# A hybrid decoder block on one core: the second 512 tokens of the gate stage in other groups, and the opening in a written order

## The chip, the cores and the metric

The kernel runs on one core of a Trainium2 chip. The time is the device time of one execution in microseconds (us), the median of several. The engines are called as in the profile: PE is the matrix engine (PEld its weight loads), DVE the vector engine, ACT the scalar engine, POOL the GpSimd engine, SP the engine from whose queue the kernel issues nearly all its DMAs. PSUM is the memory that matmuls write, SBUF the memory that all engines read and write.

## The reference

One layer on 1024 tokens of 1024 channels. What matters here is the first projection and everything behind the MLP:

```python
z = rms_norm(h, norm_mix_g[l])
proj = z @ w_in[l]
...
z = rms_norm(h, norm_ple_g[l])
gate = jax.nn.sigmoid(z @ w_ple_gate[l] + b_ple_gate[l])
h = h + gate * (p[l] @ w_ple_proj[l])
return rms_norm(h, norm_final_g)
```

w_ple_gate is 1024 x 1024, w_ple_proj 256 x 1024. All arithmetic is in 32-bit floats.

## The kernel before

Activations lie transposed: 128 channels on the partitions, tokens along the row. H[0] to H[7] are the eight blocks of the residual stream. Each operand of a matmul is split in two rounded parts, hi and lo (`split`: ACT writes hi, DVE subtracts it to get lo; for weights `load_weights` does the same and can hand the subtraction to POOL). A product is then three matmuls: hi x hi, hi x lo, lo x hi (`mm`).

The first RMS norm divides behind the matmul, since the divisor is one number per token: PE multiplies by the gain-scaled x, and the rows that drain PSUM multiply by R, the reciprocal root mean square. `Norm.add` squares a block on ACT and adds it up on DVE, `sums` adds over partitions with two matmuls by a matrix of ones (n_ps in the profile), `rstd` makes the reciprocal root.

**Opening.** For each block k of x, SP loads H[k] and 384 columns of the first weights (wl), ACT and DVE split both, and PE runs 18 matmuls into ps_l. The squares go along: blocks 0 to 2 are added at k = 2, after that one per block. The loads of two small tables (`tables`) and a chain of small DVE rows on four columns (`softplus`, tile sp) are issued at k = 2. Up to there, instructions marked by `pin` keep the order of the program; from then on (`in_order.clear()`) the scheduler chooses.

**Gate stage.** For each output block o and each group of tokens, PE runs 24 matmuls of the gate (ps_e; k over eight blocks, three products) and 6 of the projection (ps_j, or the other half of a ps_e tile). `ple_out` then drains them: DVE multiplies by R (L1055), ACT takes the sigmoid, DVE multiplies by the projection (L1061) and adds to H (L1062), and `fin.add` squares the result for the final norm (ACT, DVE). The groups are tokens 0 to 511, 512 to 767 and 768 to 1023; each runs over all eight outputs in the order of ORDER:

```python
GROUPS = (slice(0, 512), slice(512, 768), slice(768, 1024))
ORDER = ((0, 1, 2, 3, 4, 5, 6, 7), (2, 3, 4, 5, 6, 7, 0, 1), (0, 1, 4, 5, 6, 7, 2, 3))
```

In the third group, `ple_in_normed` multiplies the operand by R before it is split (DVE L928, ACT L177, DVE L178), so that the sigmoid reads PSUM itself (L1053). The gate's weights for outputs 4 to 7 stay in SBUF (wg4 to wg7 in tiles B); those of 0 to 3 go through a ring of two and are loaded and split again: 0 and 1 in the second group, 2 and 3 in the third, with the subtraction on POOL (FETCH).

`finish` forms the final norm of a group while the next one runs: `fin.sums`, `rstd`, then one DVE row per output that multiplies by gain and reciprocal root (L1079), and a store for four outputs. DONE and LAST say after which output which rows come. `finish_last` does this for the third group at the end, where ACT has already multiplied by the gain (`gain`, L1084).

An output's ps_e and ps_j take turns between one two-bank tile (two of them) and two one-bank tiles (four, which the sums also use).

Of the kernel before, what the change touches and what calls it, by code (L numbers as in the profile page):

```python
# [13 lines left out]
P = 128  # L14
S = 1024
# [7 lines left out]

SOON = 20

AHEAD = ((0,), (1, 2), (3,), ())
IN = {("P5", 2): (0, 1), ("P5", 3): (2, 3), ("P3", 0): (4, 5), ("P3", 1): (6, 7)}
LATER = ((), (0, 1), (2, 3), (4, 5), (6, 7), (), ())
GROUPS = (slice(0, 512), slice(512, 768), slice(768, 1024))
NT = D // P  # L30

ORDER = ((0, 1, 2, 3, 4, 5, 6, 7), (2, 3, 4, 5, 6, 7, 0, 1), (0, 1, 4, 5, 6, 7, 2, 3))

DONE = (((), (), (0,), (1,), (2,), (3,), (4,), (5,)), ((6,), (7,), (), (), (), (), (), ()))
LAST = ((), (), (0, 1), (2, 3), (4, 5), (6, 7), (), ())
FETCH = ((0, 1, 2, 3), (0, 1), (2, 3))
NLRU = 4
NPOOL = 4
WINDOWS = (2, 4, 8, 16)
# [18 lines left out]
def block_kernel(  # L58
# [86 lines left out]
    def f32(ap):  # L145
        return ap.bitcast(F32)
# [6 lines left out]
    def got(ps):  # L153
        if ps.shape[-1] > HALF:
            return ps.rearrange("p (b j a) -> p b a j", b=2, a=2)
        return ps.rearrange("p (j a) -> p a j", a=2)

    def by(x, ps):
        if ps.shape[-1] > HALF:
            return x.rearrange("p (b a j) -> p b a j", b=2, a=2)  # L160
        return x.rearrange("p (a j) -> p a j", a=2)

    def col(name, i):
        c = COLS[name] + i
        return vecs[:, c : c + 1]
# [3 lines left out]
    def pin(ins):  # L169
        return tc.keep_in_program_order(ins) if in_order else ins  # L170
# [3 lines left out]
    def split(src, hi, lo, g=None, eng=None):  # L174

        if g is None:
            first = pin(nc.scalar.activation(hi, src, AF.Copy))  # L177
            lowest[:] = [pin((eng or nc.vector).tensor_tensor(lo, src, f32(hi), ALU.subtract)).ins]  # L178
        else:
            first = pin(nc.scalar.activation(hi, src, AF.Identity, scale=g))  # L180
            lowest[:] = [pin(nc.vector.scalar_tensor_tensor(lo, src, g, f32(hi), ALU.mult, ALU.subtract)).ins]
        return first.ins
# [140 lines left out]
    todo += [(up_step, m, step) for m in range(NPAIR) for step in range(4)]  # L323
    todo += [(down_step, c, kind, q) for c, kind in KINDS for q in range(NQ)]
    for g, os in enumerate(FETCH):
        todo += [
            (load_weights, w_gate[o], f"wg{g}_{o}", S, nc.gpsimd if g else None) for o in os
        ]
    todo.reverse()
    asked = []  # L330

    def ask():
        if todo:
            fn, *args = todo.pop()
            asked.append(fn(*args))
# [151 lines left out]
    for _ in range(WARM):  # L487
        nc.tensor.matmul(ps_l[2][0][1][:, :HALF], heat, wide, start=True, stop=True)
    for k in range(NT):
        if k:  # L490
            if k == 3:
                ask()
            whi, wlo = weights()
        for hs in HALVES if k < 2 else (slice(0, S),):
            nc.sync.dma_start(H[k][:, hs], xT[k * P : (k + 1) * P, hs])
            if k == hs.start == 0:
                raw = raw_tile("wl0")[:, : 3 * P]
                whi, wlo = (t[:, : 3 * P] for t in weight_tiles("wl0"))
                nc.sync.dma_start(raw, w_lru[:P, :])
                pin(nc.vector.tensor_copy(whi, raw))  # L500
            split(H[k][:, hs], A[k][0][:, hs], A[k][1][:, hs], col("g_mix", k))
            if k == hs.start == 0:
                pin(nc.vector.tensor_tensor(wlo, raw, f32(whi), ALU.subtract))
        if k == 2:
            norm.add(H[0])
            norm.add(H[1])
# [412 lines left out]
    def ple_in(o, hs, norm, to=None):  # L919

        to = to or hs
        split(H[o][:, to], *z3(o, to), col("g_ple", o))
# [126 lines left out]
    def ple_out(hs, o, pg, pj, add=True, then=None):  # L1049
        t = T[3 + o % 2][:, : hs.stop - hs.start]  # L1050
        hv = H[o][:, hs]
        if hs == GROUPS[-1]:
            pin(nc.scalar.activation(by(t, pg), got(pg), AF.Sigmoid, bias=col("b_ple", o)))  # L1053
        else:
            nc.vector.tensor_tensor(by(t, pg), got(pg), by(R[:, hs], pg), ALU.mult)  # L1055
# [5 lines left out]
        nc.vector.tensor_tensor(by(e, pj), by(t, pj), got(pj), ALU.mult)  # L1061
        nc.vector.tensor_tensor(hv, hv, e, ALU.add)  # L1062
        if add:
            fin.add(H[o], hs)
# [21 lines left out]
    def finish_last(hs, end, squares):  # L1086
# [7 lines left out]
        for o in [*(o for o in range(0, NT, 2) if o != low), low]:  # L1094
            os = slice(o, o + 2)
            nc.vector.tensor_tensor(done[:, os], h_all[:, os, hs], r, ALU.mult)
            nc.sync.dma_start(out_end[:, os], done[:, os])

    for g, hs in enumerate(GROUPS):
        for n, o in enumerate(ORDER[g]):  # L1100
            pg, pj = ple_psum(g, hs, o, hs == GROUPS[-1] and n == NT - 1)
            if g == 0 and n < 2:
                ple_gate(g, hs, o, pg, n == 1)
                held.append((o, pg, pj))
                if n == 0:
                    first_sums()
                    continue
                for o, pg, pj in held:
                    ple_proj(hs, o, pj)
                for o, pg, pj in held:  # L1110
                    ple_out(hs, o, pg, pj)
            elif g == len(GROUPS) - 1 and n == NT - 1:
# [11 lines left out]
            end = g == len(GROUPS) - 1  # L1124
            if (g > 0 or n > 1) and not (end and n == NT - 1):
                ple_out(hs, o, pg, pj, not end or n < 6)
            if g == 0 and n > 0:
                for o in LATER[n - 1]:
                    ple_in(o, SECOND, norm2, GROUPS[1])
# [101 lines left out]
```

## Time and profile before

| | |
|---|---|
| median of 3 runs | 929.63 us (929.42 to 929.79) |
| the profiled execution | 930.07 us, its span 928.2 us |
| mean granted PE clock | 0.998 |
| PE busy | 916.3 us, 99% of the span |
| DVE, ACT, POOL busy | 765.9, 457.4, 14.9 us |
| opening, first gate of the gate stage, end of its last matmul | from 0, 809, 918.5 us |

A row of the timeline gives the start and the length in us, the engine, the line, the operation, what it writes and reads, the shapes, how many instructions are merged, and in brackets how long the engine was idle before it and what ended that. Matmuls overlap: the distance from start to start is their pace. A row of the waits gives who waited for whom: total us, how many times, the longest.

### The profile page before, as it was taken

How to read it: one execution, taken by the hardware profiler on the slowest of the kernel's cores; microseconds unless marked ns; L12 is line 12 of the kernel's file. 1: busy time of each engine (PE TensorE's matmuls, PEld its weight loads, DVE VectorE, ACT ScalarE, POOL GpSimd, SP SyncE). 2: the span in 40 equal slices, each digit the busy share in tenths (PEclk: the TensorE clock that was granted, in tenths of full speed). 3: DMA queues.
4: the chain of work that ended last, by engine and by line, in shares of the span. 5: the costliest groups of instructions: out<-in, count | busy, mean ns of one | idle time of the engine just before them, and what ended most of it. 6: DMA issues, size and time to landing. Idle time of an engine off the chain costs nothing.

```text
span 928.2 us, 11481 instructions
## 1 busy us (share of the span) xinstructions
PE 916.3 (99%) x4471; PEld 802.4 (86%) x4471; DVE 765.9 (83%) x930; ACT 457.4 (49%) x545; POOL 14.9 (2%) x11
## 2 busy tenths in 40 slices
PE   9999999999999999999999999999999999999996
PEld 6888888888888888888888888888888888888995
DVE  6997984669998888888888989979776679885976
ACT  7567893447543343343334654434343446653445
POOL 0000000002000000000000000000000000000220
PEclk9999999999999999999999999999999999999999
DMA  7210143211254355345434988366522441031122
GB/s 264 96 50 23 46 154 118 68 45 67 72 189 161 125 175 197 126 148 178 174 125 153 361 314 315 128 209 203 186 91 91 136 136 46 24 117 43 46 92 91
DMA packets 45333, 125.03 MB, mean 135 GB/s; under 512 B 4192, under 2 KB 6240, under 8 KB 45280
## 3 DMA queue, kind: packets, MB, share of 16 engines
q1 hardware_dynamic: 45136, 124.27, 38.4%
q8 instruction: 35, 0.57, 0.3%
q14 instruction: 18, 0.15, 0.1%
q10 hardware_dynamic: 144, 0.04, 0.0%
HBM read 90.74 MB, written 33.55 MB: 134 GB/s over the span
## 4 chain that ended last, share of the span: by engine, by line
PE 91%; DVE 5%; ACT 2%; DMA 1%; issue 0%; DVEq 0%; ACTq 0%
PE ps_P_u L351 31%; PE ps_P_d L351 31%; PE ps_i L351 10%; PE ps_o L351 9%; PE ps_e L351 6%; PE ps_l L351 2%; DVE h L1062 1%; PE ps_j L351 1%; PE ps_g L571 1%; DMA wl_raw<-in_w_lru 1%; DVE h L1079 1%; PE ps_p L351 1%; DVE t L391 1%; DVE t L1061 0%; DVE t L1055 0%; DVE a L178 0%
## 5 line engine op out<-in xcount | busy, mean ns | idle before, releaser
L351 PE MATMUL ps_P_d<-a,wd_P_hi 128*128 128x512 f32 x880 | 261.7, 379 | 0.0
L351 PEld LDWEIGHTS ps_P_d<-a,wd_P_hi 128*128 128x128 f32 x880 | 166.3, 189 | 23.6
L351 PE MATMUL ps_P_d<-a,wd_P_lo 128*128 128x512 f32 x440 | 166.8, 379 | 0.0
L351 PE MATMUL ps_P_u<-a,wu_hi 128*128 128x512 f32 x512 | 152.3, 379 | 0.0
L351 PE MATMUL ps_P_u<-y,wu_hi 128*128 128x512 f32 x384 | 114.2, 379 | 0.0
L351 PEld LDWEIGHTS ps_P_u<-a,wu_hi 128*128 128x128 f32 x512 | 96.8, 189 | 13.8
L351 PE MATMUL ps_P_u<-a,wu_lo 128*128 128x512 f32 x256 | 97.0, 379 | 0.0
L351 PEld LDWEIGHTS ps_P_d<-a,wd_P_lo 128*128 128x128 f32 x440 | 83.2, 189 | 11.8
L351 PEld LDWEIGHTS ps_P_u<-y,wu_hi 128*128 128x128 f32 x384 | 72.6, 189 | 10.3
L747 DVE TENSOR_TENSOR t<-t,ps_P_u 128x512 f32<-128x512 f32 (+1 forms) x80 | 62.6, 783 | 20.4 <-PE ps_P_u L351 20.4
L351 PE MATMUL ps_i<-a,wi_hi 128*128 128x512 f32 x288 | 74.3, 380 | 0.0
L351 PE MATMUL ps_P_u<-y,wu_lo 128*128 128x512 f32 x192 | 72.8, 379 | 0.0
L177 ACT ACTIVATE a<-wd 128x1024 fp32r<-128x1024 f32 x56 | 59.0, 1055 | 21.6 <-PE ps_P_d L351 11.6
L178 DVE TENSOR_TENSOR a<-wd,a 128x1024 fp32r<-128x1024 f32 x56 | 67.4, 1223 | 1.3 <-ACT a L177 0.9
L351 PE MATMUL ps_o<-y,wo_hi 128*128 128x512 f32 x256 | 65.7, 379 | 0.0
L351 PEld LDWEIGHTS ps_i<-a,wi_hi 128*128 128x128 f32 x288 | 54.1, 189 | 8.8 <-issue 0.7
L177 ACT ACTIVATE wu_hi<-wu 128x1024 fp32r<-128x1024 f32 x24 | 25.4, 1059 | 69.8 <-PE ps_P_u L351 44.1
L177 ACT ACTIVATE wu_hi<-wu_raw 128x1024 fp32r<-128x1024 f32 (+1 forms) x26 | 25.3, 976 | 66.3 <-PE ps_P_u L351 41.3
L351 PEld LDWEIGHTS ps_o<-y,wo_hi 128*128 128x128 f32 x256 | 48.4, 189 | 6.8
L351 PEld LDWEIGHTS ps_P_u<-a,wu_lo 128*128 128x128 f32 x256 | 48.4, 189 | 6.8
L177 ACT ACTIVATE wd_P_hi<-wd 128x1024 fp32r<-128x1024 f32 x24 | 25.3, 1055 | 47.3 <-PE ps_P_d L351 47.2
L390 ACT ACTIVATE t<-h 128x512 f32<-128x512 f32 (+2 forms) x47 | 32.8, 699 | 28.9 <-DVE h L1062 20.1
(226 smaller groups left out, 1540.6 us busy)
## 6 DMA issues: line engine op xcount, KB each, us to landing
wd<-act SPq DMA_DIRECT2D x56, 512.0 KB, 5.6
act<-t SPq DMA_DIRECT2D x32, 512.0 KB, 4.3
wu_raw<-in_w_up SPq DMA_DIRECT2D x16, 512.0 KB, 3.2
wu<-in_w_up SPq DMA_DIRECT2D x16, 512.0 KB, 3.8
act<-wu SPq DMA_DIRECT2D x16, 512.0 KB, 4.6
wd<-in_w_down SPq DMA_DIRECT2D x16, 512.0 KB, 6.3
h<-in_xT SPq DMA_DIRECT2D x14, 512.0 KB, 4.5
wg_raw<-in_w_gate SPq DMA_DIRECT2D x12, 512.0 KB, 3.2
```

What stands on the lines that cost most here:

```text
L177: first = pin(nc.scalar.activation(hi, src, AF.Copy))
L178: lowest[:] = [pin((eng or nc.vector).tensor_tensor(lo, src, f32(hi), ALU.subtract)).ins]
L351: ins = nc.tensor.matmul(ps, w, turns(z[:, hs]), start=first and z is zhi and w is whi, stop=last and w is wlo, skip_group_check=more,)
L390: pin(nc.scalar.activation(sq, t[:, hs], AF.Square))
L391: self.eng.tensor_tensor(self.acc[:, hs], self.acc[:, hs], sq, ALU.add)
L571: nc.tensor.matmul(x, w[r, o * P : (o + 1) * P], turns(z[r, at : at + HALF]), start=n == 0, stop=n == 2)
L747: (eng or nc.vector).tensor_tensor(to, to if y is None else y, x, ALU.add)
L1062: nc.vector.tensor_tensor(hv, hv, e, ALU.add)
L1079: nc.vector.scalar_tensor_tensor(hv, hv, col("g_fin", o), rfin[:, hs], ALU.mult, ALU.mult)
```

## The change

In the gate stage the groups become four: tokens 0 to 511 with all eight outputs; tokens 512 to 1023 with outputs 2, 3, 4 and 5; tokens 512 to 767 and then 768 to 1023 with outputs 6, 7, 0 and 1. The second half is no longer normalised before it is split: `ple_in` splits all 512 columns during the first group, and every drain multiplies by R. The weights of outputs 2 and 3 stay in the ring from the first to the second group, those of 0 and 1 are loaded once more, and no split is on POOL. `finish` is as before for tokens 0 to 511 (now with one, then two outputs per step in the second group, and all eight there); for 512 to 767 ACT multiplies by the gain, and DVE normalises four outputs in one row of 1024 elements.

In the opening AFTER lists which blocks' squares follow each block (0 at k = 2, 1 at k = 3, 2 and 3 at k = 4, 4 and 5 at k = 5, 6 at k = 6, 7 at k = 7), the weights' split follows the block's from k = 2 on, `tables` moves to k = 3, and the pinned order lasts to the last block.

```diff
+AFTER = (), (), (0,), (1,), (2, 3), (4, 5), (6,)
...
-GROUPS = (slice(0, 512), slice(512, 768), slice(768, 1024))
+GROUPS = (slice(0, 512), slice(512, 1024), slice(512, 768), slice(768, 1024))
...
-ORDER = ((0, 1, 2, 3, 4, 5, 6, 7), (2, 3, 4, 5, 6, 7, 0, 1), (0, 1, 4, 5, 6, 7, 2, 3))
-
-DONE = (((), (), (0,), (1,), (2,), (3,), (4,), (5,)), ((6,), (7,), (), (), (), (), (), ()))
-LAST = ((), (), (0, 1), (2, 3), (4, 5), (6, 7), (), ())
-FETCH = ((0, 1, 2, 3), (0, 1), (2, 3))
+ORDER = ((0, 1, 2, 3, 4, 5, 6, 7), (2, 3, 4, 5), (6, 7, 0, 1), (6, 7, 0, 1))
+
+DONE = ((), (0, 1, 2, 3), (4, 5), (6, 7))
+LAST = ((0, 1, 2, 3), (4, 5, 6, 7), (), ())
+FETCH = ((0, 1, 2, 3), (), (0, 1), ())
...
-        todo += [
-            (load_weights, w_gate[o], f"wg{g}_{o}", S, nc.gpsimd if g else None) for o in os
-        ]
+        todo += [(load_weights, w_gate[o], f"wg{g}_{o}") for o in os]
...
     for k in range(NT):
-        if k:
-            if k == 3:
-                ask()
+        halves = HALVES if k < 2 else (slice(0, S),)
+        if k == 1:
             whi, wlo = weights()
...
             split(H[k][:, hs], A[k][0][:, hs], A[k][1][:, hs], col("g_mix", k))
+            if k > 1:
+                whi, wlo = weights()
...
+        for i in AFTER[k] if k < len(AFTER) else (k,):
+            norm.add(H[i])
+        if k == NT - 1:
+            in_order.clear()
+            ask()
         if k == 2:
-            norm.add(H[0])
-            norm.add(H[1])
-        if k > 1:
-            norm.add(H[k])
-            in_order.clear()
-        if k == 2:
+            softplus()
+        if k == 3:
             tables()
-            softplus()
...
-    def ple_in_normed(o, hs):
-
-        z = T[1 + o % 2][:, hs]
-        nc.vector.scalar_tensor_tensor(z, H[o][:, hs], col("g_ple", o), R[:, hs], ALU.mult, ALU.mult)
-        split(z, *z3(o, hs))
...
-        if hs == GROUPS[-1]:
-            pin(nc.scalar.activation(by(t, pg), got(pg), AF.Sigmoid, bias=col("b_ple", o)))
-        else:
-            nc.vector.tensor_tensor(by(t, pg), got(pg), by(R[:, hs], pg), ALU.mult)
-            nc.scalar.activation(t, t, AF.Sigmoid, bias=col("b_ple", o))
+        nc.vector.tensor_tensor(by(t, pg), got(pg), by(R[:, hs], pg), ALU.mult)
+        pin(nc.scalar.activation(t, t, AF.Sigmoid, bias=col("b_ple", o)))
...
+        if hs != FIRST:
+            for o in os[::4]:
+                x = h_all[:, o : o + 4, hs]
+                n = hs.stop - hs.start
+                nc.vector.tensor_tensor(x, x, rfin[:, hs].unsqueeze(1).broadcast_to([P, 4, n]), ALU.mult)
+                store(slice(o, o + 4), hs)
+            return
...
             if g == 1:
-                ple_in_normed(n, GROUPS[2])
-            if end and n < 6:
                 gain(o, hs)
-            if end and n == NT - 1:
+                finish(FIRST, DONE[n])
+            if g == END - 1:
+                gain(o, hs)
+            if g == END and n < last - 1:
+                gain(o, hs)
...
-            if g > 0:
-                finish(GROUPS[0], DONE[g - 1][n])
-            if end:
-                finish(GROUPS[1], LAST[n])
+            if g == END:
+                finish(GROUPS[END - 1], LAST[n])
```

The scheduler decides where rows stand on an engine. Three places show what it made of this. The first is DVE in the opening, from the remainder of block 2 (written to a) on; sp are the small rows of `softplus`, t the additions of squares, wl the weights. Before:

```order
L181 SCALAR_TENSOR_TENSOR a_70<-h_67,vecs_137,a_70 128x1024
L464 TENSOR_SCALAR sp_146<-vecs_137 128x4
L482 TENSOR_TENSOR sp_146<-vecs_137 128x4
L465 TENSOR_TENSOR sp_146<-vecs_137,sp_146 128x4
L476 TENSOR_SCALAR sp_146<-sp_146 128x4
L391 TENSOR_TENSOR t_68<-t_68 128x1024
L467 TENSOR_SCALAR sp_146<-sp_146 128x4
L391 TENSOR_TENSOR t_68<-t_68 128x1024
L447 SCALAR_TENSOR_TENSOR recip_t_69<-ones_142 128x16
L468 RECIPROCAL sp_146<-sp_146 128x4
L178 TENSOR_TENSOR wl3_lo_289<-wl3_raw_287,wl3_hi_288 128x384
```

The same place after the change, from the fourth sp row on (lines are one lower or higher):

```order
L475 TENSOR_SCALAR sp_146<-sp_146 128x4
L466 TENSOR_SCALAR sp_146<-sp_146 128x4
L467 RECIPROCAL sp_146<-sp_146 128x4
L468 TENSOR_TENSOR sp_146<-sp_146 128x4
L469 TENSOR_TENSOR sp_146<-sp_146 128x4
L472 TENSOR_TENSOR sp_146<-sp_146 128x4
L473 TENSOR_SCALAR sp_146<-sp_146 128x4
L472 TENSOR_TENSOR sp_146<-sp_146 128x4
L182 SCALAR_TENSOR_TENSOR a_70<-h_67,vecs_137,a_70 128x1024
L473 TENSOR_SCALAR sp_146<-sp_146 128x4
L179 TENSOR_TENSOR wl3_lo_284<-wl3_raw_282,wl3_hi_283 128x384
```

The two additions of squares no longer stand ahead of block 3's remainder (L182) and weights; seven rows of the sp chain stand there one behind the other.

The second place is DVE around the operands of the sums over tokens 512 to 767 (ple9, for n3_ps512). Before, they stand in the third group, behind the last output of the second (e1_1):

```order
L1055 TENSOR_TENSOR t_68<-ps_e1_1_6626,rstd_71 128x256
L1061 TENSOR_TENSOR t_68<-t_68,ps_e1_1_6626 128x256
L1062 TENSOR_TENSOR h_67<-h_67,t_68 128x256
L391 TENSOR_TENSOR t_68<-t_68 128x256
L415 CAST ple9_5700<-t_68 128x256
L416 TENSOR_TENSOR ple9_5700<-t_68,ple9_5700 128x256
L1061 TENSOR_TENSOR t_68<-t_68,ps_j2_0_6674 128x256
```

After it they stand behind the last output of the group ahead of the last one (e2_1), and the next drain (e3_6, of the last group) is again a product with rstd:

```order
L1045 TENSOR_TENSOR t_68<-ps_e2_1_6616,rstd_71 128x256
L1051 TENSOR_TENSOR t_68<-t_68,ps_e2_1_6616 128x256
L1052 TENSOR_TENSOR h_67<-h_67,t_68 128x256
L390 TENSOR_TENSOR t_68<-t_68 128x256
L414 CAST ple9_5700<-t_68 128x256
L415 TENSOR_TENSOR ple9_5700<-t_68,ple9_5700 128x256
L1045 TENSOR_TENSOR t_68<-ps_e3_6_6654,rstd_71 128x256
```

DVE's rows are the same here; what moved is PE's place for the sums. Before, it is behind the gate of the last group's third output (e2_4):

```order
L351 MATMUL ps_j2_4_6751<-proj2_5921,proj7_5926 128x256
L351 MATMUL ps_e2_4_6750<-a_70 128x256 x24
L417 MATMUL n3_ps512_6788<-ple9_5700,ones_142 128x256
L418 MATMUL n3_ps512_6788<-ple9_5700,ones_142 128x256
L351 MATMUL ps_e2_5_6799<-proj0_5919,proj4_5923 128x256
```

After it, it is behind the gate of the last group's first output (e3_6):

```order
L350 MATMUL ps_j3_6_6655<-proj2_5921,proj7_5926 128x256
L350 MATMUL ps_e3_6_6654<-a_70 128x256 x24
L416 MATMUL n3_ps512_6693<-ple9_5700,ones_142 128x256
L417 MATMUL n3_ps512_6693<-ple9_5700,ones_142 128x256
L350 MATMUL ps_e3_7_6704<-proj0_5919,proj4_5923 128x256
```

Between the last gate that feeds the sums and the sums themselves stood three outputs of PE's work; now it is one.

More of the change, by code (lines that the diff above doesn't have):

```diff
@@ L489, in block_kernel @@
     for k in range(NT):
-        if k:
-            if k == 3:
-                ask()
+        halves = HALVES if k < 2 else (slice(0, S),)
+        if k == 1:
             whi, wlo = weights()
-        for hs in HALVES if k < 2 else (slice(0, S),):
+        for hs in halves:
             nc.sync.dma_start(H[k][:, hs], xT[k * P : (k + 1) * P, hs])
@@ L917, in z3, with ple_in @@
         return [x[:, n : n + hs.stop - hs.start] for x in pair]
-    def ple_in(o, hs, norm, to=None):
-        to = to or hs
-        split(H[o][:, to], *z3(o, to), col("g_ple", o))
+    def ple_in(o, hs, norm):
+        split(H[o][:, hs], *z3(o, hs), col("g_ple", o))
         norm.add(H[o], hs)
-    def ple_in_normed(o, hs):
-        z = T[1 + o % 2][:, hs]
-        nc.vector.scalar_tensor_tensor(z, H[o][:, hs], col("g_ple", o), R[:, hs], ALU.mult, ALU.mult)
-        split(z, *z3(o, hs))
     def down(n):
@@ L1097, in finish_last @@
             nc.sync.dma_start(out_end[:, os], done[:, os])
+    END = len(GROUPS) - 1
     for g, hs in enumerate(GROUPS):
+        last = len(ORDER[g]) - 1
+        if g == END:
+            fin.n[hs.start] = len(ORDER[1])
         for n, o in enumerate(ORDER[g]):
-            pg, pj = ple_psum(g, hs, o, hs == GROUPS[-1] and n == NT - 1)
+            end = g == END and n == last
+            pg, pj = ple_psum(g, hs, o, end)
             if g == 0 and n < 2:
@@ L1111, in block_kernel @@
                     ple_out(hs, o, pg, pj)
-            elif g == len(GROUPS) - 1 and n == NT - 1:
+            elif end:
                 ple_gate(g, hs, o, pg)
@@ L1122, in block_kernel @@
                 gate_p[n + 3] = B[n + 3]
-            end = g == len(GROUPS) - 1
-            if (g > 0 or n > 1) and not (end and n == NT - 1):
-                ple_out(hs, o, pg, pj, not end or n < 6)
+            if (g > 0 or n > 1) and not end:
+                ple_out(hs, o, pg, pj, g < END or n < last - 1)
             if g == 0 and n > 0:
                 for o in LATER[n - 1]:
-                    ple_in(o, SECOND, norm2, GROUPS[1])
+                    ple_in(o, SECOND, norm2)
                 if n == NT - 2:
@@ L1132, in block_kernel @@
             if g == 1:
-                ple_in_normed(n, GROUPS[2])
-            if end and n < 6:
                 gain(o, hs)
-            if end and n == NT - 1:
+                finish(FIRST, DONE[n])
[3 more added lines that the diff above has]
+                gain(o, hs)
+            if end:
                 prev = ORDER[g][n - 1]
@@ L1150, in block_kernel @@
                 squares += sqs
-            if g > 0:
-                finish(GROUPS[0], DONE[g - 1][n])
-            if end:
-                finish(GROUPS[1], LAST[n])
+            if g == END:
+                finish(GROUPS[END - 1], LAST[n])
     finish_last(GROUPS[-1], ORDER[-1][-1], squares)
```

## The prediction

> **What bounds the kernel now.** I read the page's busy times first, then who TensorE (PE) waits for over the whole run, then the timeline of the opening and of the last 75 us, which the change touches.
>
> ```profile
> PE 916.3 (99%) x4471; PEld 802.4 (86%) x4471; DVE 765.9 (83%) x930; ACT 457.4 (49%) x545; POOL 14.9 (2%) x11
> ...
> PE ps_e L351 <- ACT t L1053: 1.3, 1, 1.3
> ...
> PE ps_l L351 <- DVE a L181: 0.9, 2, 0.8
> ...
> PE n_ps L418 <- DVE ple L416: 0.4, 1, 0.4
> ```
>
> PE is busy for 99% of the span. The list of its waits (us in total, times, longest) has six rows in all: these, a short one in the gate stage, the first matmul's and the last sums'. So only two things can move the time: fewer or longer matmuls, and those waits. One quoted wait is in the opening (ps_l), two are in the gate stage (ps_e, n_ps). Between the two stages the change moves nothing.
>
> **Gate stage, the matmuls.** The first rows show a gate of 512 columns, then one of 256; the others show where PE stands still.
>
> ```profile
> 856.26 5.34 PE L351 MATMUL ps_e<-ple,a 128*128 128x512 f32 x24
> 861.44 0.83 PE L351 MATMUL ps_j<-proj,proj 128*128 128x256 f32 x6
> ...
> 868.81 2.84 PE L351 MATMUL ps_e<-a 128*128 128x256 f32 x24
> 871.49 0.39 PE L417 MATMUL n_ps<-ple,ones 128*128 128x512 f32 x1
> ...
> 872.69 0.83 PE L351 MATMUL ps_e<-proj,proj 128*128 128x256 f32 x6
> ...
> 877.09 2.94 PE L351 MATMUL ps_e<-a 128*128 128x256 f32 x24 [0.23 <-DVE t L1055]
> ...
> 905.69 2.94 PE L351 MATMUL ps_e<-a 128*128 128x256 f32 x24 [1.29 <-ACT t L1053]
> ...
> 917.85 0.83 PE L351 MATMUL ps_j<-proj,proj 128*128 128x256 f32 x6
> 918.52 1.06 PE L427 MATMUL n_ps<-t,ones 128*128 128x256 f32 x4
> ```
>
> From start to start, 24 matmuls of 512 columns take 861.44 - 856.26 = 5.18 us, 215.8 ns each; 24 of 256 take 871.49 - 868.81 = 2.68 us, 111.7 ns each. Two of 256 cost 7.6 ns more than one of 512. An output has 24 gate and 6 projection matmuls. The second 512 tokens take 16 x 30 = 480 matmuls of 256 now, 53.62 us; four sums of squares add 0.69 (two at 0.23, two at 0.115): 54.31 us of work. The rows give 918.52 - 861.44 = 57.08 us, so PE loses 2.77 us standing still: about 0.74 at the first sums (871.49 to 872.69 for two matmuls worth 0.46), 0.4 at 877.09, 1.5 at 905.69 (1.29 listed, the rest restarting).
>
> After the change: 4 x 30 of 512, 25.90 us; 8 x 30 of 256, 26.81; sums 0.69: 53.40 us. That is 0.91 less than 54.31, which no wait can hide, as PE sets the pace. The Trainium skill ("TensorE: Matmul & The Clock Gate", Back-to-back issue gap) has a warm matmul take N/2.4 + 2.5 ns. By it the two lengths take 215.8 and 109.2 ns, the change saves 0.3 us here instead of 0.9, and the forecast would be 0.6 us later. The 512 agrees with the trace, the 256 does not, and the measured 111.7 is what I use.
>
> **Gate stage, the waits.** These rows are DVE and POOL before the longest wait.
>
> ```profile
> 897.66 1.95 DVE L1062 TENSOR_TENSOR h<-h,t 128x256 f32<-128x256 f32 x1
> ...
> 902.40 1.88 DVE L1062 TENSOR_TENSOR h<-h,t 128x256 f32<-128x256 f32 x1
> ...
> 896.88 2.45 POOL L178 TENSOR_TENSOR wg_lo<-wg_raw,wg_hi 128x1024 fp32r<-128x1024 f32 x1 [22.38 <-ACT wg_hi L177]
> 901.63 2.37 POOL L178 TENSOR_TENSOR wg_lo<-wg_raw,wg_hi 128x1024 fp32r<-128x1024 f32 x1 [2.30 <-ACT wg_hi L177]
> ...
> 890.64 0.42 DVE L1055 TENSOR_TENSOR t<-ps_e,rstd 128x256 f32<-128x256 f32 x1
> ...
> 893.41 0.42 DVE L1055 TENSOR_TENSOR t<-ps_e,rstd 128x256 f32<-128x256 f32 x1
> ```
>
> An addition of 256 columns (0.42 us in the undisturbed rows, as other rows of two operands) takes 1.9 when it meets POOL's weight split, and ends 0.28 us after POOL does (899.61 against 899.33, 904.28 against 904.00). That makes the drains late, PE finds no free PSUM, and waits. The change takes all four splits off POOL: two are gone with their loads (outputs 2 and 3 keep their weights), two go to DVE. It also takes out DVE's eight scalings and eight subtractions for the third group, and splits 512 columns instead of 256 in the preceding stage, where two outputs of 6.5 us each lie between a drain and its PSUM's next use. ACT gains eight scalings by the final gain, in a stage where it is half idle, and DVE's eight normalisations of 256 columns become two rows of 1024; their stores stay two. On SP two weight loads fall away and none is moved past anything that is waited for. So I count the old 2.77 us of standing still as gone, and look for what is late next.
>
> It is the sums over tokens 512 to 767 (n3_ps512). In PE's order they stood behind the third gate of the last group, and now stand behind its first.
>
> The whole chain of the third group's last output (drain, sigmoid, product, addition, square, addition, cast, subtraction) now has to fit into one output's 3.35 us of PE instead of three outputs'. Its rows of before, with the 512-wide one and the last output:
>
> ```profile
> 896.35 0.29 DVE L415 CAST ple<-t 128x256 fp32r<-128x256 f32 x1
> 896.67 0.43 DVE L416 TENSOR_TENSOR ple<-t,ple 128x256 fp32r<-128x256 f32 x1
> ...
> 846.00 0.69 DVE L391 TENSOR_TENSOR t<-t 128x512 f32<-128x512 f32 x1 [0.76 <-ACT t L390]
> ...
> 889.92 0.83 PE L351 MATMUL ps_j<-proj,proj 128*128 128x256 f32 x6
> ...
> 918.05 0.47 ACT L1053 ACTIVATE t<-ps_e,vecs 128x256 f32<-128x256 f32 x1 [0.58 <-PE ps_e L351]
> ...
> 918.78 0.42 DVE L1061 TENSOR_TENSOR t<-t,ps_j 128x256 f32<-128x256 f32 x1 [0.40 <-PE ps_j L351]
> ```
>
> One 256-wide output takes DVE and ACT 893.41 - 890.64 = 2.77 us from drain to drain, 2.86 to the end of its last addition. Cast and subtraction add 0.78, the gate's end needs 0.2 to be seen: 3.85 us. PE is there 3.35 us plus one matmul of 0.11 later: it waits 0.4 us. That holds if DVE has caught up by then. A 512-wide output keeps DVE for 4 x 0.69, and group two adds eight normalisations (some 0.7 each), two splits of 1024 columns (at most 1.3 each) and the rows around two sums: 23 to 25 us in PE's 26.4. I put DVE 1.5 us behind there; group three regains 3.35 - 2.77 = 0.58 an output, 1.7 over three. Ends: 0, and 2.0 us of wait where DVE is as late as before (893.41 against 889.92, 3.3 us after the gate was readable). I take 0.4.
>
> **Tail, +0.27.** Before, the last sigmoid reads PSUM itself at 918.05, and its 0.47 lie beside the six projection matmuls, so that L1061 waits for PE (918.78, 0.93 after the gate's end). Now DVE first multiplies by rstd: 0.2 + 0.45 + 0.53 = 1.2 us. Ends: 0 and 0.5. Gate stage in all: 53.40 + 0.4 - 57.08 + 0.27 = **-3.0 us**.
>
> **The opening.** The order written out moves H[3] ahead of the small tables' loads, and each weight split behind its block's split. PE's rows, DVE's and ACT's:
>
> ```profile
> 18.01 0.59 PE L351 MATMUL ps_l<-a,wl_hi 128*128 128x512 f32 x2
> 19.36 0.70 PE L351 MATMUL ps_l<-a,wl_hi 128*128 128x512 f32 x2 [0.76 <-DVE a L181]
> ...
> 34.57 0.40 PE L417 MATMUL n_ps<-hl,ones 128*128 128x512 f32 x1
> ...
> 35.28 0.39 PE L418 MATMUL n_ps<-hl,ones 128*128 128x512 f32 x1
> 35.51 1.03 PE L351 MATMUL ps_l<-a,wl_hi 128*128 128x512 f32 x4
> ...
> 11.90 0.56 DVE L178 TENSOR_TENSOR wl_lo<-wl_raw,wl_hi 128x384 fp32r<-128x384 f32 x1 [0.92 <-ACT wl_hi L177]
> 12.94 1.28 DVE L181 SCALAR_TENSOR_TENSOR a<-h,vecs,a 128x1024 fp32r<-128x1024 f32 x1 [0.48 <-ACT a L180]
> ...
> 22.23 0.16 DVE L473 TENSOR_TENSOR sp<-sp 128x4 f32<-128x4 f32 x1
> 22.31 1.22 DVE L391 TENSOR_TENSOR t<-t 128x1024 f32<-128x1024 f32 x1
> ...
> 34.04 0.71 DVE L416 TENSOR_TENSOR hl<-t,hl 128x512 fp32r<-128x512 f32 x1
> 34.64 0.18 DVE L473 TENSOR_TENSOR sp<-sp 128x4 f32<-128x4 f32 x1
> 34.85 0.17 DVE L474 TENSOR_SCALAR sp<-sp 128x4 f32<-128x4 f32 x1
> ...
> 8.79 1.41 ACT L180 ACTIVATE a<-h,vecs 128x512 fp32r<-128x512 f32 x2
> ...
> 11.77 1.13 ACT L180 ACTIVATE a<-h,vecs 128x1024 fp32r<-128x1024 f32 x1
> ...
> 15.65 0.19 ACT L466 ACTIVATE sp<-sp 128x4 f32<-128x4 f32 x1
> ```
>
> The two small loads that H[3] passes on SP are first used behind the sums of squares, so that costs nothing. Block 3's remainder no longer stands behind two additions of squares: PE's gap goes, 19.36 - (18.01 + 2 x 0.216) = 0.92 us. But in a row of its own each sp step waits for the last, 0.21 us (34.64 to 34.85) instead of the 0.08 that it costs between others (22.23 to 22.31). What is late next is the two sums of squares, which PE runs before the last block. Before, DVE worked without a pause from 12.94 until their last operand at 34.75, 21.8 us, and PE used it at 35.28: 0.53 us of slack. After: ACT can split block 2 between 10.20 (it is free) and about 11.35 (the block is loaded ahead of the weights whose split of half a microsecond DVE waits for at 11.90), say 10.75, so DVE starts at 10.75 + 1.13 = 11.9. It adds the split that stood ahead (0.5), five sp rows that came later (0.4) and the serial chain (seven steps and the exponential's 0.19 between: 0.9): 11.9 + 21.8 + 1.8 = 35.5 to 35.6. PE could be there at 35.28 - 0.92 = 34.36. It waits instead, and runs its last sum at 35.63: **+0.35 us**. Ends: -0.92 (DVE early enough) and +1.0 (ACT starting at 11.35, and a little more serial time).
>
> **The sum.** -3.0 + 0.35 = -2.65 us. The profiled execution took 930.07 us (span 928.2, 1.87 around it); it becomes 927.4. It lies 0.44 above the median of 929.63, so the forecast is 929.63 - 2.65 = **927.0 us**.
>
> **Rivals.** (1) *The opening pays*: DVE's remainders come early enough, no wait at the sums, -0.92 instead of +0.35: 925.7. For it: block 3 does arrive earlier. Against: DVE had no idle time left there. Chance 0.18. (2) *DVE stays behind* by before's 3.3 us into group three, regains 1.7, and the second sums wait 2.0 us: 927.0 + 1.6 = 928.6. For it: 512-wide drains, normalisation and two splits now share 26 us. Chance 0.13. (3) *Slower*: the long additions were not POOL's doing but the pace of drain, square and gain together, 902.40 - 897.66 = 4.74 us an output. Group three then falls 1.39 us behind per output: 1.5 + 3 x 1.39 = 5.7 us at the second sums, 927.0 + 5.7 = 932.7. The saving is gone from a lag of 2.65 us (3.73 us an output), and it is slower beyond doubt from 4.5 (4.35 us). Against: the two long rows end with POOL's, and 2.77 us was reached where POOL was still. Chance 0.08.
>
> **Numbers.** My forecast 0.56, rivals 0.18, 0.13, 0.08, anything else 0.05. A measurement here tells 0.2%, 1.86 us, from no change: faster is below 927.77, slower above 931.49. My case lies on the faster side nearly wholly (0.52), with rival 1 and 0.03 of rival 2 and the rest: 0.73. Same: 0.04, most of rival 2, part of the rest: 0.18. Slower: 0.09. The range 925.2 to 928.9 takes in rivals 1 and 2 and the ends of the opening; it leaves out rival 3 and extremes.
>
> **What would show it.** Right: no POOL work after the opening; no DVE addition of 256 columns over 0.5 us; PE without a gap at 18 us but with one of 1 to 2 us before the sums at about 35; the last projection about 3 us earlier; PE short of 0.5 us at the second sums. Wrong: sums starting at 33.6 (rival 1), or PE waiting over 1.5 us behind the first gate of the last group (rivals 2, 3).

## The result and the profile after

After: 927.21 us, median of 11 runs (926.47 to 927.82). Before, on the same chip: 929.44 us (929.24 to 929.86). The ratio is 0.9975 with a 95% interval of 0.9966 to 0.9984, so the kernel is 2.2 us faster; 927.0 was forecast. The profiled execution after has a span of 925.4 us (928.2 before).

The busy times, then PE's waits below the first matmul's:

```profile
PE 915.3 (99%) x4351; PEld 798.5 (86%) x4351; DVE 758.8 (82%) x903; ACT 456.5 (49%) x531; POOL 5.6 (1%) x7
...
PE n_ps L416 <- DVE hl L414: 0.6, 1, 0.6
PE n_ps L417 <- DVE hl L415: 0.4, 1, 0.4
PE n_ps L426 <- DVE t L1153: 0.4, 1, 0.4
PE n_ps L426 <- ACT t L1146: 0.3, 1, 0.3
```

PE has 120 matmuls fewer. The wait of 1.3 us in the gate stage and the two on ps_l in the opening are gone. In their place PE waits in the opening for the operands of the sums of squares (1.0 us), which is the wait that the forecast put there. The other two are in the tail. POOL's 5.6 us are its rows at the start and three on weights (wu) at 213 to 219 us; in the gate stage it does nothing.

The timeline of PE, first around the opening's sums, then in the gate stage (the first projection of the second 512 tokens, the second sums, the last projection):

```profile
33.80 0.49 PE L416 MATMUL n_ps<-hl,ones 128*128 128x512 f32 x1 [0.55 <-DVE hl L414]
34.74 0.50 PE L417 MATMUL n_ps<-hl,ones 128*128 128x512 f32 x1 [0.44 <-DVE hl L415]
...
35.68 1.02 PE L350 MATMUL ps_l<-a,wl_hi 128*128 128x512 f32 x4
...
861.46 1.46 PE L350 MATMUL ps_j<-proj,proj 128*128 128x512 f32 x6
...
904.69 0.36 PE L416 MATMUL n_ps<-ple,ones 128*128 128x256 f32 x1
905.06 0.39 PE L417 MATMUL n_ps<-ple,ones 128*128 128x256 f32 x1
905.28 0.83 PE L350 MATMUL ps_e<-proj,proj 128*128 128x256 f32 x6
...
914.66 0.83 PE L350 MATMUL ps_j<-proj,proj 128*128 128x256 f32 x6
```

The last projection starts 53.20 us behind the first one of this half; before it was 917.85 - 861.44 = 56.41. From there to the end of the span it takes 10.74 us, before 10.35. Together, from the first projection of the second half to the end: 63.94 us instead of 66.76, **-2.82 us**. This distance doesn't depend on the opening and is used below for all kernels; a span is given to 0.1 us, so a hundredth means nothing in it.

DVE and ACT, first an addition of a drain, then the last output:

```profile
902.88 0.42 DVE L1052 TENSOR_TENSOR h<-h,t 128x256 f32<-128x256 f32 x1
...
914.86 0.43 DVE L1045 TENSOR_TENSOR t<-ps_e,rstd 128x256 f32<-128x256 f32 x1 [0.58 <-PE ps_e L350]
...
915.32 0.51 ACT L1046 ACTIVATE t<-t,vecs 128x256 f32<-128x256 f32 x1 [1.32 <-DVE t L1045]
...
915.86 0.42 DVE L1051 TENSOR_TENSOR t<-t,ps_j 128x256 f32<-128x256 f32 x1 [0.57 <-ACT t L1046]
```

No addition of 256 columns is longer than 0.43 us. The last product starts 1.20 us behind the start of the last projection, 0.93 before.

### The profile page after: what moved, and what is told of

Same layout as the page of the kernel before. It is cut to its first block, busy times and chain, and to the rows that moved or that the text cites. A ratio compares the mean times of both kernels' runs of the same rounds, so it can differ in the third digit from the quotient of the medians.

```text
span 925.4 us, 11180 instructions
## 1 busy us (share of the span) xinstructions
PE 915.3 (99%) x4351; PEld 798.5 (86%) x4351; DVE 758.8 (82%) x903; ACT 456.5 (49%) x531; POOL 5.6 (1%) x7
## 4 chain that ended last, share of the span: by engine, by line
PE 95%; DVE 2%; issue 1%; DMA 1%; SPq 0%; ACT 0%; DVEq 0%
PE ps_P_d L350 31%; PE ps_P_u L350 31%; PE ps_i L350 10%; PE ps_e L350 10%; PE ps_o L350 9%; PE ps_j L350 1%; DMA h<-in_xT 1%; PE ps_g L571 1%; PE ps_p L350 1%; DVE t L390 1%; PE ps_l L350 0%; DVE wl_lo L179 0%; PE n_ps L417 0%; DVE t L1093 0%; DVE a L182 0%
## 5 line engine op out<-in xcount | busy, mean ns | idle before, releaser
L350 PEld LDWEIGHTS ps_P_d<-a,wd_P_hi 128*128 128x128 f32 x880 | 166.3, 189 | 23.6
```

The costliest lines, as they stand in the source:

```text
L350: ins = nc.tensor.matmul(ps, w, turns(z[:, hs]), start=first and z is zhi and w is whi, stop=last and w is wlo, skip_group_check=more,)
```

## Experiments

The kernel before took 929.4 to 929.5 us in all sets of runs; ratios are to it. Stage times are distances in the traces.

### e1: the opening's order alone

Before with the opening's part of the diff (AFTER, the place of the weights' split, `tables`, `in_order.clear()`), gate stage as before.

> The kernel before with the opening's new order alone. My theory: PE's 0.92 us gap at 18 us goes, but DVE delivers the operands of the sums of squares later, PE waits there, and PE leaves the opening within -0.2 to +0.5 us of before: 929.4 to 930.0 against 929.5. Rival 1 (the opening pays): no wait at the sums, -0.9 us: 928.6.

Measured: 929.88 us, ratio 1.0007 (0.9998 to 1.0015), 0.46 above the kernel before. PE's sums of e1:

```profile
33.70 0.49 PE L418 MATMUL n_ps<-hl,ones 128*128 128x512 f32 x1
34.63 0.50 PE L419 MATMUL n_ps<-hl,ones 128*128 128x512 f32 x1 [0.44 <-DVE hl L417]
...
35.57 1.02 PE L352 MATMUL ps_l<-a,wl_hi 128*128 128x512 f32 x4
```

PE's gap at 18 us is gone and comes back in front of the sums. The opening brings nothing. Rival 1 of the prediction falls.

### e2: the gate stage alone

After with the opening of before.

> The changed gate stage alone, with the opening as before. My theory: all of the gain is here, -3.0 us in PE's own rows (0.91 by the longer matmuls, 2.77 by waits gone, 0.4 and 0.27 given back): 926.4 to 926.8. Rival 1: about -2 us, since the opening would carry the other part: 927.4.

Measured: 926.75 us, ratio 0.9970 (0.9959 to 0.9982). From the first projection of the second half to the end 64.02 us, 2.74 less than before. All of the gain is in the gate stage, and e2 is 0.46 us below after, as e1 was above before: two pairs that agree on what the opening costs, though 0.46 alone is within their intervals. e2's median is a weak one: three of its runs took 926.26 to 926.34 us, the other three 927.16 to 927.20, and it lies between them.

### e3: before without POOL

```diff
-            (load_weights, w_gate[o], f"wg{g}_{o}", S, nc.gpsimd if g else None) for o in os
+            (load_weights, w_gate[o], f"wg{g}_{o}", S) for o in os
```

Groups of 256 columns, four splits, normalised third group and opening are as before; only the four subtractions go from POOL to DVE.

> The kernel before, with the four weight splits of the gate stage on DVE instead of POOL, nothing else. My theory (POOL's splits stretch DVE's rows beside them): no DVE addition of 256 columns over 0.5 us; most of the 2.77 us of standing PE goes although DVE has 4 x 1.2 us more to do: -1.3 to -2.5 us, 927.0 to 928.2. Rival 3 (the long additions are the drain's own pace): they stay, and the time is 929.5 or later by the added DVE work.

Measured: 926.49 us, ratio 0.9969 (0.9956 to 0.9981): 0.7 us below after's median, with overlapping intervals, so at least as fast as the whole change, and more than I expected. PE at the start of the second half, at the first sums and at the end:

```profile
860.60 0.83 PE L351 MATMUL ps_j<-proj,proj 128*128 128x256 f32 x6
...
870.64 0.39 PE L417 MATMUL n_ps<-ple,ones 128*128 128x512 f32 x1
...
871.11 0.83 PE L351 MATMUL ps_e<-proj,proj 128*128 128x256 f32 x6
...
914.23 0.83 PE L351 MATMUL ps_j<-proj,proj 128*128 128x256 f32 x6
914.90 1.06 PE L427 MATMUL n_ps<-t,ones 128*128 128x256 f32 x4
```

914.90 - 860.60 = 54.30 us, within a hundredth the work that the prediction counted for the old groups (54.31): PE no longer stands still between these rows, neither at the sums nor for the drains. All 2.77 us of standing were POOL's doing, also those that I had thought might be DVE's own lateness. From the first projection to the end it is 64.00 us, 2.76 less, as in after; what e3 is ahead of after lies in front of this stage (its first projection starts at 860.60, after's at 861.46). Rival 3, that drain, square and gain together set the pace, falls: DVE does the four weight splits as well here, and PE waits for none of it.

### e4: after, its two splits back on POOL

```diff
-        todo += [(load_weights, w_gate[o], f"wg{g}_{o}") for o in os]
+        todo += [(load_weights, w_gate[o], f"wg{g}_{o}", S, nc.gpsimd if g else None) for o in os]
```

> The changed kernel with its two remaining weight splits back on POOL. My theory: the two DVE rows that meet them grow to about 2 us; they stand in the group of 512 columns, where PE has 6.5 us an output, so PE waits 0 to 0.5 us: 927.2 to 927.7. Rival (DVE has no slack in that group): every microsecond that DVE loses, 2 to 3 us, comes back as waiting: 929 to 930.

Measured: 927.17 us, ratio 0.9978 (0.9968 to 0.9987); 64.01 us to the end against 63.94. The first of the two splits on POOL and the addition that meets it:

```profile
868.88 2.37 POOL L179 TENSOR_TENSOR wg_lo<-wg_raw,wg_hi 128x1024 fp32r<-128x1024 f32 x1 [650.31 <-ACT wg_hi L178]
...
870.53 1.26 DVE L1052 TENSOR_TENSOR h<-h,t 128x512 f32<-128x512 f32 x1
```

The addition is stretched (1.26 us; of 512 columns, 0.69 undisturbed), and so is the one that meets the second split (1.64 us), but here an output lasts 6.47 us on PE, and PE waits for no drain. The stretching is the same, its price here is zero: it reached PE only in the kernel before, with 256 columns, 3.35 us an output and four splits.

### e7: the second group's gates in halves

After, with the 96 gate matmuls of 512 columns issued as 192 of 256. The rest is as after, but for the order of addresses in which this group's drain reads its operands.

```diff
-        for k in range(NT):
-            zhi, zlo = z3(k, hs)
-            mm(
-                [(slice(0, hs.stop - hs.start), pg)], kblk(whi, k), kblk(wlo, k), zhi, zlo,
...
+        wide = hs.stop - hs.start
+        cut = 256 if g else wide
+        for n in range(0, wide, cut):
+            for k in range(NT):
+                zhi, zlo = z3(k, hs)
+                mm(
+                    [(slice(n, n + cut), pg[:, n : n + cut])], kblk(whi, k), kblk(wlo, k), zhi, zlo,
...
```

> The kernel after, with the 96 gate matmuls of 512 columns of the second group issued as 192 of 256 columns (first half of the tokens, then second half, into one PSUM; projections, drains and everything else as after, one drain reads its operands in another order of address). It measures what the longer matmuls are worth by themselves. By the durations of the rows before (215.8 ns against 2 x 111.7) it is 96 x 7.6 ns = 0.73 us slower than after, 927.9 us, with the group's gates 5.36 us apart from projection to projection instead of 5.18. By the Trainium skill's formula (page TensorE: Matmul & The Clock Gate, Back-to-back issue gap: 2.5 ns a matmul) it is 0.24 us slower. If weight loads stand in the way (one load for every matmul of 256 columns), both are too low, and the gates are further apart than 5.4 us.

Measured: 927.77 us, ratio 0.9981 (0.9972 to 0.9990), 0.56 above after. One output of the group:

```profile
861.25 1.46 PE L350 MATMUL ps_j<-proj,proj 128*128 128x512 f32 x6
867.91 1.46 PE L350 MATMUL ps_e<-proj,proj 128*128 128x512 f32 x6
...
888.33 0.83 PE L350 MATMUL ps_j<-proj,proj 128*128 128x256 f32 x6
```

6.66 us instead of 6.47 for this one. All four, with the sums between them, take 888.33 - 861.25 = 27.08 us, in after 887.82 - 861.46 = 26.36: 0.72 more (64.75 us to the end against 63.94). The rows' 0.73 holds, the 0.24 of the formula does not. The medians' 0.56 is within their intervals.

### e6: the second sums one output later

```diff
-LAST = ((0, 1, 2, 3), (4, 5, 6, 7), (), ())
+LAST = ((), (0, 1, 2, 3), (4, 5, 6, 7), ())
```

> The kernel after, with the final sums of tokens 512 to 767 taken one output later (behind the second gate of the last group). My theory: the whole change loses 0.48 us there (gate's end 904.57, projection 905.28, two matmuls of 0.115 us between them), because the chain of the third group's last output has one output's PE time and needs a little more. One output later it has 3.35 us more, so PE passes without a wait: 0.45 us faster than after, 926.7 to 926.8 us. Rival: the wait comes from how close the drains of both groups stand on DVE, and moves with the sums, or the normalisation and store then come too late for the end: then no change, or up to 0.5 us slower.

Measured: 926.85 us, ratio 0.9972 (0.9961 to 0.9983); 63.90 us to the end. PE, then two rows of DVE:

```profile
907.77 0.29 PE L416 MATMUL n_ps<-ple,ones 128*128 128x256 f32 x1
...
908.01 0.83 PE L350 MATMUL ps_j<-proj,proj 128*128 128x256 f32 x6
...
914.04 0.83 PE L350 MATMUL ps_j<-proj,proj 128*128 128x256 f32 x6
...
916.98 0.70 PE L426 MATMUL n_ps<-t,ones 128*128 128x256 f32 x2 [0.33 <-DVE t L1153]
...
912.97 1.22 DVE L1071 TENSOR_TENSOR h<-h,t 128x1024 f32<-128x1024 f32 x1
...
915.58 0.42 DVE L1051 TENSOR_TENSOR t<-t,ps_j 128x256 f32<-128x256 f32 x1
```

The wait is gone from the sums: they take 0.24 us, and the last projection comes 0.46 us sooner after the first (52.74 us, 53.20 in after). But DVE's second normalisation of 1024 elements (912.97) now stands between the drains of the last two outputs; in after it starts at 909.91. The last product (915.58) starts 1.54 us behind the last projection instead of 1.20, and the last sums (916.98) 2.94 instead of 2.59: 0.35 of the 0.46 is given back, 0.11 is left. The medians are 0.36 apart, within their intervals, and don't decide between the two. The wait was real; the rival was right that the normalisation then comes too late for the end.

### e12: the last output without its product with rstd, e11: after again

For the last output the sigmoid reads PSUM itself; the product with rstd is left out there.

```diff
+        if hs == GROUPS[-1] and o == ORDER[-1][-1]:
+            pin(nc.scalar.activation(by(t, pg), got(pg), AF.Sigmoid, bias=col("b_ple", o)))
+        else:
...
```

> The kernel after, with the last output's sigmoid reading PSUM directly; its multiplication by rstd is left out, so that output of the last 256 tokens is gated without it. It measures the tail's term. My theory: that multiplication stands on the path that sets the end; without it ACT starts 0.46 us earlier, and the product waits for the projection instead (as before: 0.93 us behind the gate's end, now 1.20): 0.27 us faster than after by that row, at most 0.39 by the whole tail (10.74 us from the last projection to the end, 10.35 before): 926.8 to 926.95 us. Rival: the sums of the last but one output or the normalisation of the group before bind in the tail; then no change.

> The kernel after itself, on the same chip as these, as the base for e9, e10 and e12: 927.2 us, as measured at first.

Measured: e11 927.23 us (ratio 0.9977, 0.9966 to 0.9987), e12 926.97 us (0.9972, 0.9962 to 0.9982). The last output of e12:

```profile
914.71 0.83 PE L350 MATMUL ps_j<-proj,proj 128*128 128x256 f32 x6
914.91 0.47 ACT L1046 ACTIVATE t<-ps_e,vecs 128x256 f32<-128x256 f32 x1 [0.86 <-PE ps_e L350]
...
915.63 0.42 DVE L1054 TENSOR_TENSOR t<-t,ps_j 128x256 f32<-128x256 f32 x1 [1.31 <-PE ps_j L350]
```

The product starts 0.92 us behind the start of the last projection, 1.20 in after, and from the last projection to the end it is 10.49 us, in e11 10.76: -0.27. The last sums show the same to the hundredth: they start 2.32 us behind the last projection (917.03), in e11 2.59. The tail's term is what the prediction said; the medians (-0.26) are within each other's intervals and don't add to it.

### e5, e8, e9, e10: softplus out of the opening

If DVE is what the sums wait for, taking the sp rows away there must bring the sums forward. e5 calls `softplus` just ahead of the first scan of the LRU stage, e9 right behind the opening's rstd; e8 and e10 do the same to e3 with the change's opening.

```diff
-        if k == 2:
-            softplus()
...
+    softplus()
     lru_scan(0, last)
```

> The kernel after, with the softplus of the LRU's parameters (the sp steps) moved out of the opening to just ahead of the first scan. My theory: in the opening DVE is what the two sums of squares wait for; the sp steps take 1.2 us in a row (13.67 to 14.88) and some 0.08 each later, about 2 us in all, and PE stands still for about 1.6 us around the sums (33.1 to 35.68, with four matmuls of 0.23 us in it). Without them DVE is 2 us earlier, and the sums start behind the matmuls ahead of them: 1.2 to 1.6 us faster than after, 925.6 to 926.0 us beside 927.2, with the first projection (ps_i) about 1.4 us earlier. Rival: the sums are late because the last block arrives late, or ACT is late; then DVE only gets idle time ahead of its last rows, and the time stays at 927.2. Second rival: the small rows, now in the LRU stage, hold DVE up there, each waiting 0.2 us for the one before; then part or all of the gain is lost again, at most 16 x 0.2 = 3.2 us.

> The kernel before with its four gate weight splits on DVE (as e3, 926.49 us) and the change's order in the opening, with the softplus moved to just ahead of the first scan (as e5). The regrouping of the gate stage is not in it. If the two add: 926.5, plus 0.45 us for the opening's order by e1, less 1.4 us for the softplus by my theory of e5: about 925.5 us, faster than both kernels and than any part tried. If softplus gives nothing: 926.5 to 926.9.

> The kernel after, with the softplus of the LRU's parameters called right behind the opening's rstd instead of inside the opening. e5 had it just ahead of the first scan: the sums of squares then no longer waited (first sum at 32.90, first projection at 37.78 instead of 39.56), but the sp steps stood in a row on the path to the first scan and PE lost 3.3 us in the LRU stage. Here the order on DVE puts them one by one between rows of 1024 columns (0.08 us each by the rows of the opening, about 2 us in all), long before the scan. My theory: the opening keeps its 1.6 to 1.8 us, and DVE is about 1.3 us later at the scan than in e5 without its sp steps, of which PE's slack there, worked out from e5 as about 2.4 us less the 1.7 that PE is earlier, hides about half: 1.0 to 1.5 us faster than after, 925.7 to 926.2 us. Rival: the opening's wait only moves: DVE is busy without a pause from 38 to 72 us, so what PE gains at the sums it loses again at the LRU's gates; then 927.2 us, with PE's wait on ps_g as long as the sums' was (1 to 1.7 us).

> The kernel before with its four gate weight splits on DVE (as e3, 926.5 us) and the change's order in the opening, with the softplus right behind the opening's rstd (as e9); the gate stage is not regrouped. It tells whether the regrouping is needed once POOL is out. By adding: 926.5, +0.45 for the opening's order (e1), -1.0 to -1.5 (theory of e9): 925.4 to 926.0 us, no slower than e9. If regrouping is worth its 0.9 us in spite of e3: 0.5 to 0.9 us slower than e9.

Measured: e5 931.97 us (ratio 1.0025, 1.0016 to 1.0034), e8 931.99 (1.0027, 1.0018 to 1.0036), e9 931.80 (1.0025, 1.0015 to 1.0034), e10 932.54 (1.0034, 1.0021 to 1.0048): all slower, where I had expected the fastest of all. PE of e5, in the opening and at the LRU's gates (ps_g), and the windows around these gates (PE busy, then the other engines; PEclk is the granted clock):

```profile
32.90 0.40 PE L416 MATMUL n_ps<-hl,ones 128*128 128x512 f32 x1
...
33.90 1.02 PE L350 MATMUL ps_l<-a,wl_hi 128*128 128x512 f32 x4
...
95.65 0.48 PE L569 MATMUL ps_g<-y,hl 64*128 64x512 f32 x1
99.26 0.48 PE L569 MATMUL ps_g<-y,hl 64*128 64x512 f32 x2 [3.13 <-ACT t L642]
...
100.00:102.00 2.00, 2.00 (x10) 1.27 (x11) 2.00 (x2) 2.00 (x3) 0.00 (x0) 0.67 0.00 0
102.00:104.00 2.00, 2.00 (x6) 1.55 (x6) 1.97 (x2) 2.00 (x3) 0.00 (x0) 0.50 0.04 8
```

The opening did as the theory has it: the sums follow the matmuls without a wait, and the last block starts at 33.90 instead of 35.68. So DVE's sp rows are the cause of the wait in the opening. But the gain is lost three times over at the LRU's gates. There the sp steps stand in a row, 25 of them at 0.2 us each (83.97 to 88.96), and the chain of the profile that leads to these gates runs through them all to ACT's rows of the scan. PE waits 3.3 us for ACT, and behind that wait its clock is halved until 104: 2 x 0.33 + 2 x 0.50 = 1.7 us of PE's time in the two windows. The twelve ps_g and the projections up to ps_p took 24.01 us in after (97.42 to 121.43) and take 29.71 (95.65 to 125.36): 5.7 us more, of which 3.3 are the wait and 1.7 the clock; the other 0.7 isn't traced. My bound of 3.2 us for this rival counted 16 steps instead of 25, and left the clock out.

e9 was meant to keep the sp rows off that way. It didn't test this alone: the scheduler also moved the LRU's first gates ahead of a projection. PE of e9 there, and its windows:

```profile
49.86 0.70 PE L569 MATMUL ps_g<-y,hl 64*128 64x512 f32 x2 [0.64 <-ACT y L178]
51.19 2.77 PE L569 MATMUL ps_g<-y,hl 64*128 64x512 f32 x10 [0.63 <-DVE y L179]
54.80 1.22 PE L350 MATMUL ps_i<-a,wi_lo 128*128 128x512 f32 x2 [0.85 <-DVE wi_lo L179]
...
54.00:56.00 2.00, 1.20 (x3) 1.02 (x4) 2.00 (x5) 1.99 (x3) 0.00 (x0) 0.57 0.20 27
56.00:58.00 2.00, 2.00 (x7) 1.61 (x6) 2.00 (x5) 1.96 (x4) 0.00 (x0) 0.57 0.62 236
```

In after these gates come at 60.37. In e9 PE reaches them at 49, waits three times, for ACT and for DVE, which is busy all the time, and its twelve gates (1.5 us in after) last until 54.80. From the window at 54 on it has 0.57 of its clock for two windows, again 1.7 us of its time. From the last block to the second pair's gates it takes 5.6 us more than after (33.95 to 113.32 against 35.68 to 109.47). Whether what the opening gains in these four (0.9 to 1.6 us, by the distance that is used under Opening below) can be kept at all stays open. e8 and e10, with the old groups, are as slow as e5 and e9 and have the same loss of clock (0.66 and 0.50 from 100 to 104 in e8, 0.76 and 0.50 from 54 to 58 in e10), so this has nothing to do with the gate stage.

## Why the prediction was right, point by point

- **Standing still of PE, -2.77:** right. e3 takes POOL's splits away and nothing else, and the trace gives -2.76, with no wait left up to the last sums. The mechanism (a DVE row that ends behind POOL's) is seen again in e4, 0.54 and 0.55 us behind it. The prediction shows two of before's four splits on POOL. The other two (866.81 to 869.39, 872.09 to 874.50) stretch a subtraction and a scaling of the third group's operand, the first two rows below, both to 0.29 us behind POOL's end. These stand ahead of the first sums' operand and of the drain that PE waits for at 877.09, so those waits are POOL's too, as e3 shows by their absence. The Trainium skill ("SBUF — State Buffer", SBUF: two separate sides) says that DVE with two SBUF inputs and GpSimd arbitrate for one pair of ports, held for a whole instruction, and that the other fully blocks; the additions of 0.42 us that took 1.9 agree. So do two products with one operand in PSUM that ran beside POOL's two splits of before (896.88 to 899.33, 901.63 to 904.00) at full pace, the last two rows below; DVE in the kernel before:

```profile
867.50 2.18 DVE L178 TENSOR_TENSOR a<-t,a 128x256 fp32r<-128x256 f32 x1
...
872.20 2.59 DVE L928 SCALAR_TENSOR_TENSOR t<-h,vecs,rstd 128x256 f32<-128x256 f32 x1
...
897.20 0.42 DVE L1061 TENSOR_TENSOR t<-t,ps_j 128x256 f32<-128x256 f32 x1
...
901.95 0.42 DVE L1061 TENSOR_TENSOR t<-t,ps_e 128x256 f32<-128x256 f32 x1 [2.33 <-ACT t L1053]
```

- **Longer matmuls, -0.91:** right in size. e7 gives 0.72 us for the 96 gate pairs in the rows (0.73 by the row's 7.6 ns); the 24 projection pairs were not tried apart. The 0.3 that the prediction worked out by the Trainium skill's formula ("TensorE: Matmul & The Clock Gate", Back-to-back issue gap) is not what the rows show; the page gives the formula for an isolated matmul and says itself that it counts too little at small N.
- **Second sums, +0.4:** 904.57 (the last gate's end, by the pace) to 905.28 is 0.71 for 0.23 us of work: +0.48. e6 shows that it is the distance of one output, and also that removing it leaves only 0.11 at the last sums. Rival 2 falls: the wait was 0.5, not 2.0.
- **Tail, +0.27:** right for the last product (1.20 against 0.93, and e12 gives back 0.27). The whole tail is 0.39 longer: 0.27 up to the last sums, which start 2.59 us behind the last projection (before 2.32). DVE's last normalisation follows them at 2.28 us in both kernels; the other 0.1 lies behind it, among the stores, where the prediction had no term, and its cause is open.
- **Gate stage, -3.0:** -2.82 in the trace, -2.7 in e2's medians. The difference to the forecast is 0.1 at the sums and 0.1 in the tail.
- **Opening, +0.35:** right in sign and cause (e1, e5), too small. The loads move the whole opening from one execution to the next (ACT's split of block 1 starts between 7.69 and 8.79), so its length is taken from the start of that split to the start of PE's last block. With the old order it is 26.72 to 26.78 us (before, where the split starts at 8.79, e2 and e3), with the new one 27.41 to 27.45 (after, e1, e4, e6, e7, e11 and e12). Rows of after, then of e2:

```profile
8.23 1.38 ACT L181 ACTIVATE a<-h,vecs 128x512 fp32r<-128x512 f32 x2
...
7.69 1.42 ACT L180 ACTIVATE a<-h,vecs 128x512 fp32r<-128x512 f32 x2 [0.46 <-DMA h<-in_xT]
...
34.47 1.02 PE L349 MATMUL ps_l<-a,wl_hi 128*128 128x512 f32 x4
```

  So the new order costs 0.7 us at PE's last block for the same start, and both orders pass a late start on in full. Some 0.5 is left at the first projection of the second 512 tokens (853.21 to 853.41 us behind the split, 852.65 to 852.89 with the old order), and the medians say +0.46 twice. The two profiles of the change hide it (35.51 and 35.68), since before's split started 0.56 us later than after's. The term that was too small is DVE's work from block 2's remainder to the last operand: 21.8 + 1.8 = 23.6 us by the forecast, 23.9 in after (11.37 to 35.29).
- **Sum:** -2.65 forecast, -2.23 measured, inside the range. The forecast's time is 0.2 us off, its difference 0.4: the time came closer by luck, since the three runs that it starts from have a median 0.19 us above the eleven of the comparison.

What the prediction didn't see is how the gain is composed. It counted 2.77 of waits and 0.91 of matmuls as two gains. e3 shows that the first needs one line. The regrouping then adds 0.91, and its own sums and tail take back 0.48 and 0.39: nothing is left of it. In the traces e3 and after differ by 0.06 us in the gate stage, which is nothing at this precision. e3's expectation went wrong on the size: it left part of the waiting to DVE, which turned out to be POOL's too.

## What to carry to other kernels

Ask of each wait which single row makes it late before rebuilding the stage: here one argument that moved four subtractions from POOL to DVE is worth as much as the new groups, at 926.49 us (e3) against 926.75 (e2, with the same opening). A gain in the pace of matmuls has to be set against the waits that a shorter distance between producer and sums creates, and against the tail. Moving small dependent rows out of a full stretch pays only if they don't land on the way of another engine; look at the order there, since a scheduler may move much else.

## What the runs showed of the hardware

- A wait of PE can cost more than its length. In e5, behind a wait of 3.1 us, the granted clock is 0.67 and 0.50 in the two stretches of 2 us from 100 to 104. In e9, where PE's gates come in pieces between waits of 0.64, 0.63 and 0.85 us, it is 0.57 from 54 to 58. Each loss is worth 1.7 us of PE's time. Behind the single wait of 1.3 us before, and behind those of 0.55 and 0.44 us in the opening after, the granted clock stays at 1.00 (windows of 1 and 2 us from 904 to 910 and from 33 to 40). The Trainium skill ("TensorE: Matmul & The Clock Gate", Why this matters for your kernels) warns of idle gaps of over some 3 us. e5 agrees with that; e9 shows the clock halved where no listed wait reaches 1 us, but several lie close together.
- The small dependent rows of sp cost DVE 0.2 us each when they stand alone, as in e5's chain below, against 0.08 between long rows:

```profile
84.17 0.18 DVE L467 RECIPROCAL sp<-sp 128x4 f32<-128x4 f32 x1
84.38 0.16 DVE L468 TENSOR_TENSOR sp<-sp 128x4 f32<-128x4 f32 x1
```
